# A hybrid decoder layer on one core: the order of its first column blocks, of a unit's two halves, of two norms, and the places of its tiles

## The chip, the cores and the metric

The kernel runs on one core of one Trainium2 chip. The metric is the device time of one execution in microseconds: the median of three runs before the change is 1334.2 us (1333.42 to 1334.41).

## What is computed

One layer on 256 tokens of 2048 channels, all in float32. `proj = rmsnorm(x) @ w_in` has columns for a gated-DeltaNet group (8 heads of 128: q, k, v through a causal convolution of width 4 and SiLU, a gate z, and b and a that give beta and the decay) and for a MoBA attention group (8 heads; with 256 tokens there is one block, so it is causal attention with a relative bias). The parts that the change touches:

```
q, k = l2norm(q), l2norm(k)                  # per head and token, over 128 channels
A    = tril(beta * (k k^T) * decay, -1);  T = (I + A)^-1
o_a  = rmsnorm(gated_delta_rule(q, k, v)) * silu(z);   o_b = rmsnorm(attention)
x    = x + concat(o_a, o_b) @ w_out
x    = x + cross_attention(rmsnorm(x), rmsnorm(mem))   # 4 heads, 256 memory tokens
h    = rmsnorm(x)
x    = x + (silu(dwconv3(h @ w_gate) + b) * (h @ w_up)) @ w_down      # 5632 wide
out  = rmsnorm(x)
```

## The kernel before

**Streams and units.** All weights pass one stream: a transfer on SP's queue brings a pair of units into one of three buffers `raw` (`load_pair`, line 250), and `prep` (260) splits each unit into a rounded part `hi` (ScalarE, a copy to fp32r) and a rest `lo` (VectorE, a subtraction), each in one of four tiles. `stream` (276) walks over the units, splits up to three ahead (one ahead until all of xT is there), and issues the unit's matmuls in five steps, between which `Jobs.tick` (157) may issue pieces of other work. Activations are kept channel-major as `xT`: per channel tile 256 columns of the rounded part and 256 of the rest.

A product of three terms (hi x hi, hi x rest, lo x hi) replaces each fp32 product. In a `w_unit` (296) the weights are stationary: eight matmuls of 512 columns, `hi` against both halves of an `xT` tile, then eight of 256 columns, `lo` against the rounded half. A `w_block` (325) is two such units, 16 channel tiles, and ends in an evacuation job that is added when its last `lo` matmul is issued. In an `s_block` (344) the activations are stationary and `hi` and `lo` are the moving tiles: three matmuls per channel tile and half of the tokens.

**The order of the stream** is written out from line 1144 on: the column block z0 (400 columns: b, a and three heads of z; lines 1146 and 1160), then for each head the K block and one pair of units of z1 (384 columns) or z2 (256), then Q with the MoBA values (512 columns), V with the first MoBA heads, the other MoBA heads, the keys of the memory, `w_out`, the cross-attention, the FFN in two halves of gate, up and down. The first two units of z0 hold one channel tile each, all others two.

**The jobs' order** comes from a plan: `Plan` (49) keeps a modelled time for each engine, a job is ticked when its last result is due, and evacuations wait while ScalarE or VectorE are over 3 us ahead. Tiles come from `Slots`: 14 work tiles `T`, 4 of 512 columns `T5`, 8 PSUM banks, of which side work leaves two free. On the chip each engine runs what was issued to it in that order, and semaphores make it wait.

**What the steps touch.** `start_job` (1244): splits the 16 tiles of x into `xT`, with their loads on SP's queue apart from the weight pairs (`load_x`, 1221); it loads x a second time, token-major, into `xn` (1257), squares it on ScalarE and gets the first norm r1, on which `row1` and all of the first evacuations wait. `conv_front` (555): sum of the two halves, scaling by `row1`, the convolution and SiLU, with two T tiles. `k_evac` (580): squares k on ScalarE, sums it over channels with two fp32 matmuls against `ones` (two recorded passes each) and makes the products k k^T in the same bank (597 to 601). `q_evac` (683), `v_evac` (735), `kb_evac` (829; it waits for all of U ahead of its logits), `out_norm` (711). `x_rstd` (907) sums squares over channels for the later norms. `sml` (207) holds all small parameters, those of the FFN's convolution included. When the cross-attention is over, the pool `pm` is closed and `pf` opens in its place (1325), with a filler of 96 columns ahead of `actT`.

**Where tiles lie.** The tiles of a pool lie one behind another in the order in which they are made, each rounded up to 32 bytes per partition, the pools one behind another. In the program of before, `hi0` begins at byte 45,056 of its partition, `lo0` at 61,440, `xT` at 77,824, the pool `pm` at 155,264, `oTg` at 196,224, `oTm0` at 220,800, `mT0` at 155,264 and `actT` at 155,648.

Of the kernel before, what the change touches and what calls it, by code (L numbers as in the profile page):

```python
# [16 lines left out]
P = 128  # L17
# [14 lines left out]
ZH = ((0, 3), (3, 6), (6, 8))  # L32


G_MIX, G_MEM, G_X, G_F = 0, 16, 32, 48
G_GDN, G_MOBA, C_GDN, C_FFN, B_FFN = 64, 65, 66, 66 + 96, 66 + 96 + 132
SMALL = B_FFN + FB
# [3 lines left out]
TW = 260  # L41
FILL = 96
# [136 lines left out]
class Unit:  # L179
    def __init__(self, n, ticks, after=None):  # L180
        self.n, self.ticks, self.after = n, ticks, after
# [3 lines left out]
def layer_kernel(ctx: ExitStack, tc: tile.TileContext, ins, out):  # L185
# [31 lines left out]
    stats = p0.tile([P, 640], F32, name="stats")  # L217
# [3 lines left out]
    aux = Slots(plan, [], spare=2)  # L221
# [12 lines left out]
    def stat(w, tag=None):  # L234
        _n[0] += w
        assert _n[0] <= 640
        return stats[:, _n[0] - w:_n[0]]
# [12 lines left out]
    def load_pair():  # L250
        i = state["dma"]
        if i < len(pairs):
            ap, us = pairs[i]
            n = sum(u.n for u in us)
            for a, b in ((0, us[0].n), (us[0].n, n)) if i == 0 else ((0, n),):
                sp.dma_start(raw[i % NRAW][:, a:b], ap[:, a:b])
                state[i] = state.get(i, sp.due)
            state["dma"] = i + 1

    def prep():  # L260
# [6 lines left out]
        was, plan.cur = plan.cur, Job(None, state[u.pair])  # L267
# [8 lines left out]
    def stream(upto):  # L276
        while state.setdefault("run", 0) < upto:
            i = state["run"]
            u = units[i]
            while state["prep"] <= i:  # L280
                if state[u.pair] > plan.now + AHEAD:
                    jobs.idle()
                else:
                    prep()
            plan.wait(u.due)
            for t in u.ticks:
                while (state["prep"] < min(len(units), i + 1 + (LA if (1, KT - 1) in box else 1)) and
                       state.get(units[state["prep"]].pair, 1e9) <= plan.now + AHEAD):
# [7 lines left out]
    def w_unit(src, steps):  # L296

        def high(lo_, hi_):
            def f(u):
                for j in range(lo_, hi_):  # L300
# [3 lines left out]
                    ps, w, xk = b["ps"], slice(j * P, (j + 1) * P), src(k)  # L304
                    if b["wide"]:
                        mm(ps, u.hi[:, w], xk, start=k == 0, stop=False)
                    else:
                        mm(ps[:, :256], u.hi[:, w], xk[:, :256], start=k == 0, stop=False)
                        mm(ps[:, :256], u.hi[:, w], xk[:, 256:], start=False, stop=False)
            return f  # L310

        def low(lo_, hi_):
            def f(u):
                for j in range(lo_, hi_):
                    b, k = steps[j]
                    last = k == b["k"] - 1
                    mm(b["ps"][:, :256], u.lo[:, j * P:(j + 1) * P], src(k)[:, :256], start=False, stop=last)
                    if last:
# [143 lines left out]
    def decay_job():  # L462
        ba = box["ba"].rearrange("p (b c) -> p b c", b=2)
        w = [stat(16, f"sp{i}") for i in range(6)]
# [35 lines left out]
        aux.put(ps)  # L500
        scr = dram.tile([16, P], F32, name="grow")
# [53 lines left out]
    def conv_front(ps, blk, taps, dst_fn):  # L555
# [20 lines left out]
        dst = dst_fn()  # L576
        act.activation(dst, a, AF.Silu)
        return t1, dst

    def k_evac(h):  # L580
        def f(ps):
            if "kt" not in box:
# [4 lines left out]
                box["sub"] = pm.tile([P, 2048], F32, tag="M0", name="sub")  # L587
                sp.dma_start(box["sub"][:, 1024:1536], ins["cst"][:, K_X:K_X + 512])
                box["scr"] = dram.tile([4, 2, H, 32, 32], F32, name="lscr")
                pool.memset(c[:, 2048:], 0.0)  # L590
            st = gst[h]
            t1, kT = yield from conv_front(ps, h, 4, lambda: box["kt"][:, h, :])
            act.activation(t1[:, :256], kT, AF.Square)
            yield
            while ("d", h) not in box:
                yield
            ps = yield from aux.get()
# [6 lines left out]
            vec.tensor_scalar(st[:, 0:2], ps[:, 384:386], EPS, None, op0=OP.add)  # L604
# [78 lines left out]
    def q_evac(h):  # L683
        def f(ps):
            st = gst[h]
            qT = yield from T.get()
            t1, _ = yield from conv_front(ps, 8 + h, 4, lambda: qT[:, :256])
            act.activation(t1[:, :256], qT[:, :256], AF.Square)
            yield
            while ("L", h) not in box:  # L690
                yield
            kT = box["kt"][:, h, :]
# [18 lines left out]
    def out_norm(ps, st, c_in, f_of, sink, g, z=None):  # L711

        t = yield from T.get()
# [21 lines left out]
    def v_evac(h):  # L735
        def f(ps):
            st = gst[h]
            v = yield from T.get()
            t1, _ = yield from conv_front(ps, 16 + h, 4, lambda: v[:, :256])
            T.put(t1)  # L740
# [37 lines left out]
            T.put(v)  # L778
# [23 lines left out]
            yield from out_norm(ps, st, 14, f_of, sink, gcol(G_GDN, 0), [d[:, 384:], l[:, 384:512]])  # L802
# [26 lines left out]
    def kb_evac(h):  # L829
        def f(ps):  # L830
# [3 lines left out]
            while ("qb", h) not in box or not done["bt"] or done["U"] < H:  # L834
# [25 lines left out]
            while h >= H // 2 and done["y"] < H:  # L860
                yield
            ps = yield from aux.get()
# [23 lines left out]
            yield from out_norm(ps, st, 4, f_of, sink, gcol(G_MOBA, 0))  # L886
# [19 lines left out]

    def x_rstd(ver):
# [14 lines left out]
        for tb in range(2):  # L922
            for i in range(2):
                mm(ps[:, tb:tb + 1], a[:, i * 256 + tb * P:i * 256 + (tb + 1) * P], ones[:, :1],
                   start=i == 0, stop=i == 1)
# [8 lines left out]
    def natural_ss(src, tile, ss):  # L934

        for i in range(8):
# [3 lines left out]
            plan.cur.end = sp.due  # L940
# [117 lines left out]
    def gate_evac(j):  # L1058
        def f(ps):
# [6 lines left out]
            w = sml[:, C_FFN + j * 3:C_FFN + j * 3 + 3]  # L1066
# [7 lines left out]
            act.activation(a, a, AF.Silu, bias=gcol(B_FFN, j))  # L1074
# [71 lines left out]
    def z_pairs(n):  # L1146
        us_ = s_block(xs(1), list(range(KT)), ZW[n], z_evac(n), first=0 if n else 2)
# [329 lines left out]
```

## Time and profile before

| | |
|---|---|
| runs, us | 1333.42, 1334.41, 1334.2; median 1334.2 |
| the profiled execution, us | 1333.4; its span 1331.6 |
| mean granted TensorE clock | 0.997 |
| TensorE busy, matmuls | 1316.2 us (99%) |
| VectorE, ScalarE, GpSimd busy | 938.4 (70%), 688.9 (52%), 54.7 us (4%) |
| moved by DMA | 252.53 MB, mean 190 GB/s |

Matmuls overlap in their recorded lengths: a matmul's end is modelled, and the next starts before it. What one matmul costs in a run is therefore read from start to start. All instructions bear line 96, that of a helper, so groups are told apart by their tiles: `xT,hi` is a matmul with xT moving and hi stationary. A matmul on plain fp32 tiles is recorded as two passes.

### The profile page before, as it was taken

The page shows a single profiled execution, that of the slowest core. Times are in us where ns is not written, and L with a number is a line of the kernel's source. Part 1 is how long each engine was busy: PE and PEld are TensorE (multiplying, and loading weights), DVE is VectorE, ACT ScalarE, POOL GpSimd, SP SyncE. Part 2 cuts the span into 40 slices and gives each one's busy share as a digit, 9 for nine tenths or more (in the row PEclk, how much of TensorE's full clock was granted, in tenths as well). Part 3 has the DMA queues.
Part 4 walks back from the last instruction along what each step waited for, and adds up shares of the span by engine and source line. Part 5 has one row for each costly group of instructions (what it writes and reads, how often), then busy time and mean ns, then how long its engine had stood idle before and what let it go on. Part 6 is the DMA issues. An engine that isn't in the chain of part 4 may idle for free.

```text
span 1331.6 us, 19353 instructions
## 1 busy us (share of the span) xinstructions
PE 1316.2 (99%) x7382; PEld 1147.1 (86%) x7382; DVE 938.4 (70%) x1602; ACT 688.9 (52%) x1106; POOL 54.7 (4%) x140
## 2 busy tenths in 40 slices
PE   8999999999999999999999999999999999999997
PEld 8998888888788889998888888888888888888886
DVE  5688789867686666688877777545577777775554
ACT  5776554557665454565544444443344444444443
POOL 0101000202111000000000000000000000000000
PEclk9999999999999999999999999999999999999999
DMA  9665655624355654354555666555555555555552
GB/s 332 226 226 200 226 186 190 194 80 151 123 181 191 234 193 172 145 209 167 196 192 193 200 207 205 196 197 190 189 190 190 189 190 189 190 190 190 190 190 95
DMA packets 68202, 252.53 MB, mean 190 GB/s; under 512 B 29011, under 2 KB 33292, under 8 KB 40844
## 3 DMA queue, kind: packets, MB, share of 16 engines
q1 hardware_dynamic: 66560, 247.64, 52.6%
q0 software_dynamic: 448, 2.11, 0.5%
q10 hardware_dynamic: 1100, 1.54, 0.4%
q8 instruction: 58, 0.95, 0.3%
q14 instruction: 36, 0.29, 0.1%
HBM read 246.53 MB, written 2.64 MB: 187 GB/s over the span
## 4 chain that ended last, share of the span: by engine, by line
PE 68%; issue 0%; DVE 0%; ACT 0%; POOLq 0%; POOL 0%; ACTq 0%; DVEq 0%
PE bank L96 68%; ACT xn L96 0%; DVE tt L96 0%; DVE xT L96 0%; DVE xn L96 0%; POOLq L1473 0%; POOL stats L96 0%; DVE oTx L96 0%; DVE lo L96 0%; ACT oTx L96 0%; ACTq L96 0%; DVE xres L96 0%; DVE stats L96 0%; DVEq L96 0%
## 5 line engine op out<-in xcount | busy, mean ns | idle before, releaser
L96 DVE TENSOR_TENSOR lo<-raw,hi 128x1024 fp32r<-128x1024 f32 (+4 forms) x449 | 539.9, 1204 | 315.2 <-ACT hi L96 304.9
L96 ACT ACTIVATE hi<-raw 128x1024 fp32r<-128x1024 f32 (+4 forms) x449 | 466.9, 1041 | 434.2 <-PE bank L96 329.7
L96 PE MATMUL bank<-xT,hi 128*128 128x512 f32 x2112 | 541.9, 395 | 1.4 <-DVE xT L96 1.4
L96 PEld LDWEIGHTS bank<-xT,hi 128*128 128x128 f32 x2112 | 377.8, 189 | 70.7 <-issue 2.6
L96 PEld LDWEIGHTS bank<-xT,lo 128*128 128x128 f32 x2112 | 288.0, 190 | 20.1 <-issue 0.6
L96 PE MATMUL bank<-xT,lo 128*128 128x256 f32 x2112 | 300.6, 284 | 0.0
L96 PE MATMUL bank<-hi,actT 128*128 128x512 f32 x704 | 216.9, 389 | 0.0
L96 PEld LDWEIGHTS bank<-hi,actT 128*128 128x128 f32 x704 | 132.0, 188 | 27.5
L96 PE MATMUL bank<-lo,actT 128*128 128x512 f32 x352 | 136.9, 389 | 0.0
L96 PE MATMUL bank<-hi,xT 128*128 128x512 f32 (+3 forms) x320 | 87.0, 356 | 3.5 <-ACT xT L96 2.7
L96 DVE SCALAR_TENSOR_TENSOR t<-pad,sml,t 128x256 f32<-128x256 f32 x160 | 78.2, 489 | 7.8
L96 PEld LDWEIGHTS bank<-lo,actT 128*128 128x128 f32 x352 | 66.1, 188 | 13.6
L96 ACT ACTIVATE t<-bank 128x256 f32<-128x256 f32 (+1 forms) x164 | 56.9, 350 | 26.0 <-PE bank L96 26.0
L96 PEld LDWEIGHTS bank<-hi,xT 128*128 128x128 f32 x320 | 57.7, 193 | 9.1 <-ACT xT L96 3.4
L96 DVE TENSOR_TENSOR t<-bank,t 128x256 f32<-128x256 f32 x132 | 55.0, 416 | 9.7 <-ACT t L96 9.7
L96 PE MATMUL bank<-lo,xT 128*128 128x512 f32 (+3 forms) x160 | 56.3, 352 | 0.0
L96 POOL TENSOR_TENSOR stats<-stats,pw 128x2 f32<-128x2 f32 (+1 forms) x38 | 29.0, 762 | 563.9 <-DVE stats L96 563.9
L96 ACT ACTIVATE actT<-t 128x256 fp32r<-128x256 f32 x44 | 18.2, 413 | 51.4 <-DVE t L96 51.3
L96 ACT ACTIVATE t<-t,sml 128x256 f32<-128x256 f32 x44 | 22.2, 506 | 38.9 <-DVE t L96 38.3
L96 DVE TENSOR_TENSOR t<-t,t 128x256 f32<-128x256 f32 x96 | 41.0, 427 | 1.8
L96 PEld LDWEIGHTS bank<-lo,xT 128*128 128x128 f32 x160 | 30.7, 192 | 2.6
L96 PE MATMUL bank<-oTg,hi 128*128 128x512 f32 x128 | 32.4, 395 | 0.0
(156 smaller groups left out, 984.4 us busy)
## 6 DMA issues: line engine op xcount, KB each, us to landing
raw<-wst SPq DMA_DIRECT2D x212, 1024.0 KB, 4.8
raw<-wz SPq DMA_DIRECT2D x4, 768.0 KB, 4.1
raw<-wz SPq DMA_DIRECT2D x3, 800.0 KB, 8.2
xn<-x SPq DMA_DIRECT2D x4, 512.0 KB, 10.1
raw<-wz SPq DMA_DIRECT2D x4, 512.0 KB, 4.3
tt<-mem SPq DMA_DIRECT2D x8, 256.0 KB, 5.1
tt<-memT SPq DMA_DIRECT2D x8, 256.0 KB, 5.1
xres<-xT SPq DMA_DIRECT2D x4, 512.0 KB, 5.7
```

The costliest lines, as they stand in the source:

```text
L96: r = f(o, *a, **k)
```

## The change

- **Constants and places.** The FFN's convolution weights and biases leave `sml` (338 columns become 162) for a tile `smf` of their own, loaded on GpSimd's queue when `pf` opens, ahead of `fg`. `stats` shrinks from 640 columns to 516 and is followed by a filler of 4 columns; the filler of 96 ahead of `actT` goes.
- **First columns.** z0 and z1 are interleaved unit by unit at the head of the stream, with four single-tile units each; z2's four pairs follow every second K block. Each x tile is loaded just ahead of the pair of weights that is loaded with it.
- **Turned units.** The second unit of a block runs its `lo` matmuls first; in the blocks whose halves are interleaved (memory keys, `w_out`, the first two FFN pairs) only that of every second block.
- **First norm** from squares of the channel-major x, added up and summed over channels by four one-column matmuls; the token-major load goes.
- **Norm of k** from the diagonal of k k^T: two VectorE instructions with `ident` that sum along rows, in place of the square and the two one-column matmuls.
- `conv_front` works in one T tile, jobs get their second one later; MoBA heads wait for U after their softmax and not before it; side work leaves one bank free, not two.

```diff
-SMALL = B_FFN + FB
+SMALL = C_GDN + 96
+C_FFN, B_FFN = 0, 132
+SMALL_F = B_FFN + FB
-TW = 260
-FILL = 96
+TW, STATS = 260, 516
+FILL = 4
...
-    stats = p0.tile([P, 640], F32, name="stats")
+    stats = p0.tile([P, STATS], F32, name="stats")
+    p0.tile([P, FILL], F32, name="fill")
...
-    aux = Slots(plan, [], spare=2)
+    aux = Slots(plan, [], spare=1)
...
             ap, us = pairs[i]
-            n = sum(u.n for u in us)
-            for a, b in ((0, us[0].n), (us[0].n, n)) if i == 0 else ((0, n),):
+            if i < len(x_with):
+                was, plan.cur = plan.cur, None
+                load_x(*x_with[i])
+                plan.cur = was
+            for part in [us[:1], us[1:]] if i < 2 else [us]:
+                a, b = part[0].off, part[-1].off + part[-1].n
                 sp.dma_start(raw[i % NRAW][:, a:b], ap[:, a:b])
...
         n = len(steps)
         cuts = [0, (3 * n) // 8, (6 * n) // 8, n]
-        return Unit(n * P, [high(a, b) for a, b in zip(cuts, cuts[1:])] + [low(0, n // 2), low(n // 2, n)])
-    def w_block(src, evac, wide=True):
+        hs, ls = [high(a, b) for a, b in zip(cuts, cuts[1:])], [low(0, n // 2), low(n // 2, n)]
+        return Unit(n * P, ls + hs if turn else hs + ls)
+    def w_block(src, evac, wide=True, turn=True):
         b = {"k": KT, "wide": wide, "evac": evac}
-        return [w_unit(src, [(b, k) for k in range(i, i + 8)]) for i in (0, 8)]
+        return [w_unit(src, [(b, k) for k in range(i, i + 8)], turn and i > 0) for i in (0, 8)]
...
-            t1, kT = yield from conv_front(ps, h, 4, lambda: box["kt"][:, h, :])
-            act.activation(t1[:, :256], kT, AF.Square)
+            kT = box["kt"][:, h, :]
+            t1 = yield from conv_front(ps, h, lambda: kT)
+            T.put(t1)
...
-            for tb in range(2):
-                mm(ps[:, 384 + tb:385 + tb], t1[:, tb * P:(tb + 1) * P], ones[:, :1])
             mm(ps[:, :256], kT[:, :P], kT)
             mm(ps[:, 256:384], kT[:, P:], kT[:, P:])
             yield
+            for tb in range(2):
+                stt(t1[:, tb * P:(tb + 1) * P], ps[:, tb * 256:tb * 256 + P], 1.0, ident, OP.mult, OP.mult,
+                    accum_out=st[:, tb:tb + 1])
...
-            while ("qb", h) not in box or not done["bt"] or done["U"] < H:
+            while ("qb", h) not in box or not done["bt"]:
...
-            while h >= H // 2 and done["y"] < H:
+            while done["U"] < H or (h >= H // 2 and done["y"] < H):
                 yield
...
-    for p_ in z_pairs(0):
+    for p_ in z_pairs([u for two in zip(z_units(0, Z1), z_units(1, Z1)) for u in two], 0):
         pair(*p_)
-    zp = z_pairs(1) + z_pairs(2)
+    zp = z_pairs(z_units(2, 0), KT * (ZW[0] + ZW[1]))
     for h in range(H):
         put(w_block(xs(1), k_evac(h)))
-        for p_ in zp[h:h + 1]:
+        for p_ in zp[h // 2:h // 2 + 1] if h % 2 == 0 else ():
             pair(*p_)
...
-    b = [w_block(osrc, resid_evac(n, 2, G_X, True)) for n in range(KT)]
+    b = [w_block(osrc, resid_evac(n, 2, G_X, True), turn=n % 2 > 0) for n in range(KT)]
...
+    x_with = [(0, 1), (1, 2), (2, 3), (3, 4)] + [(k, k + 2) for k in range(4, KT, 2)]
...
             if k == 11:
                 act.dma_start(sml, ins["small"])
-                xn = pm.tile([P, 2, D], F32, tag="C", name="xn")
-                for n in range(4):
-                    c = slice(n * 512, (n + 1) * 512)
-                    sp.dma_start(xn[:, :, c], ins["x"].rearrange("(b p) d -> p b d", p=P)[:, :, c])
+            if k % 2:
+                t = yield from T5.get()
...
+                    act.activation(t, xraw[:, k - 1:k + 1, :].rearrange("p b c -> p (b c)"), AF.Square)
+                    yield
+                    vec.tensor_tensor(sq, sq, t, op=OP.add)
+                    T5.put(t)
...
+        ps = yield from acc.get()
+        token_sums(ps, sq)
...
     pf = ctx.enter_context(tc.tile_pool(name="pf", bufs=1))
-    pf.tile([P, FILL], F32, name="fill")
     box["actT"] = pf.tile([P, HB, 512], F32R, name="actT")
     fg = pf.tile([P, D], F32, name="fg")
+    box["smf"] = pf.tile([P, SMALL_F], F32, name="smf")
+    pool.dma_start(box["smf"], ins["smallf"])
```

## Rows read from the trace of the kernel before

**Rows 1.** The page's first part: busy time of each engine, its share of the span, and its number of instructions.

```profile
PE 1316.2 (99%) x7382; PEld 1147.1 (86%) x7382; DVE 938.4 (70%) x1602; ACT 688.9 (52%) x1106; POOL 54.7 (4%) x140
```

**Rows 2.** Busy time by stage, in four stretches: from the first column block to its end, the K stage, the stage of Q and of the MoBA values, and the stage of V with the attention heads. Columns: stretch (us), its length, then busy us and number of instructions of TensorE's matmuls, of its weight loads, of VectorE, ScalarE and GpSimd, the granted TensorE clock (1.00 is 2.4 GHz), the mean busy share of the DMA engines, and GB/s.

```profile
5.50:29.08 23.58, 20.19 (x96) 19.23 (x97) 15.77 (x27) 14.92 (x25) 0.00 (x0) 0.93 0.98 355
29.08:106.16 77.08, 77.08 (x473) 70.34 (x473) 57.41 (x134) 50.82 (x89) 6.43 (x15) 1.00 0.67 240
106.16:207.76 101.60, 101.60 (x547) 87.95 (x545) 86.13 (x161) 58.14 (x101) 9.32 (x21) 1.00 0.56 195
207.76:393.50 185.74, 185.74 (x1136) 158.69 (x1135) 144.20 (x332) 114.46 (x263) 25.74 (x44) 1.00 0.44 153
```

**Rows 3.** The timeline of TensorE's matmuls over the first 30 us. Columns: start (us), length with the modelled end (us), engine, helper line, operation, output and operands (moving first, then stationary), array size, columns, number of matmuls merged, and in brackets the idle time before them with what ended it.

```profile
5.50 1.23 PE L96 MATMUL bank<-hi,xT 128*128 128x400 f32 x2
...
6.75 0.52 PE L96 MATMUL bank<-hi,xT 128*128 128x400 f32 x2
...
7.29 0.52 PE L96 MATMUL bank<-hi,xT 128*128 128x400 f32 x2
...
11.21 0.45 PE L96 MATMUL bank<-hi,xT 128*128 128x400 f32 x1 [2.67 <-ACT xT L96]
...
12.37 0.45 PE L96 MATMUL bank<-hi,xT 128*128 128x400 f32 x1 [0.71 <-DVE xT L96]
...
29.08 2.02 PE L96 MATMUL bank<-xT,hi 128*128 128x512 f32 x8
```

**Rows 4.** The timeline of TensorE's matmuls (columns as before): first the first and the last start of a run of 24 matmuls of 256 columns in the third column block, then the first and the last start of a run of 18 matmuls of 512 columns in the down projection.

```profile
75.06 0.40 PE L96 MATMUL bank<-hi,xT 128*128 128x256 f32 x2
...
77.94 0.63 PE L96 MATMUL bank<-xT,hi 128*128 128x512 f32 x2
...
909.82 0.39 PE L96 MATMUL bank<-lo,actT 128*128 128x512 f32 x1
...
913.90 0.39 PE L96 MATMUL bank<-lo,actT 128*128 128x512 f32 x1
```

**Rows 5.** The timeline of TensorE's matmuls in the FFN's gate and up blocks: the start of one unit, of its second half, and of the unit three further on.

```profile
821.17 2.00 PE L96 MATMUL bank<-xT,hi 128*128 128x512 f32 x8
823.02 1.11 PE L96 MATMUL bank<-xT,lo 128*128 128x256 f32 x8
...
829.55 2.00 PE L96 MATMUL bank<-xT,hi 128*128 128x512 f32 x8
```

**Rows 6.** The timeline of TensorE's matmuls in the output projection: a unit on oTm, the start of the next unit and of its second half, and the unit four after the first.

```profile
431.76 2.02 PE L96 MATMUL bank<-oTm,hi 128*128 128x512 f32 x8
...
434.56 2.03 PE L96 MATMUL bank<-oTm,hi 128*128 128x512 f32 x8
436.42 1.12 PE L96 MATMUL bank<-oTm,lo 128*128 128x256 f32 x8
...
443.00 1.31 PE L96 MATMUL bank<-oTg,hi 128*128 128x512 f32 x5
```

**Rows 7.** The timeline of ScalarE around 9 us, and then busy time, clock and DMA of three short stretches (columns as in the rows by stage).

```profile
9.13 0.87 ACT L96 ACTIVATE hi<-raw 128x800 fp32r<-128x800 f32 x1 [2.88 <-DMA raw<-wz]
...
0.00:12.00 12.00, 7.70 (x31) 6.48 (x31) 4.25 (x11) 5.80 (x10) 0.20 (x4) 1.00 0.81 262
...
8.35:11.21 2.86, 0.19 (x3) 0.00 (x1) 1.18 (x2) 2.08 (x4) 0.00 (x0) 1.00 1.01 392
...
14.00:16.00 2.00, 2.00 (x7) 1.98 (x7) 2.00 (x5) 1.57 (x3) 0.00 (x0) 0.50 1.04 396
```

**Rows 8.** Groups of instructions on VectorE and ScalarE, shapes kept apart. Columns: line, engine, operation, output and operands, shapes, count, busy us, mean ns of one, and idle time before them with what ended it.

```profile
L96 DVE TENSOR_TENSOR lo<-raw,hi 128x800 fp32r<-128x800 f32 x7 | 6.8, 990 | 4.4 <-ACT hi L96 4.3
L96 DVE TENSOR_TENSOR tt<-tt,tt 128x512 f32<-128x512 f32 x14 | 9.5, 681 | 0.0
L96 DVE SCALAR_TENSOR_TENSOR AB<-bank,stats,AB 128x128 f32<-128x128 f32 x16 | 5.5, 341 | 0.0
L96 ACT ACTIVATE hi<-raw 128x800 fp32r<-128x800 f32 x7 | 6.0, 867 | 4.7 <-DMA raw<-wz 3.6 <-PE bank L96 0.9
```

**Rows 9.** DMA issues of the page: output and source, queue, count, KB of each, and median us from issue to landing.

```profile
xn<-x SPq DMA_DIRECT2D x4, 512.0 KB, 10.1
```

**Rows 10.** The timeline of TensorE's matmuls: first a head's k work inside a K block, then the sums over channels ahead of the FFN.

```profile
96.88 0.50 PE L96 MATMUL bank<-ones,t 128*128 128x1 f32 x4
97.24 0.90 PE L96 MATMUL bank<-kt 128*128 128x256 f32 x4
97.89 0.71 PE L96 MATMUL bank<-xT,hi 128*128 128x512 f32 x2
...
609.40 0.94 PE L96 MATMUL bank<-ones,tt 128*128 128x1 f32 x8
610.21 0.96 PE L96 MATMUL bank<-xT,lo 128*128 128x256 f32 x6
```

**Rows 11.** The timeline of TensorE's matmuls in the first column block: two starts that lie 24 matmuls apart.

```profile
20.39 0.53 PE L96 MATMUL bank<-hi,xT 128*128 128x400 f32 x2
...
24.74 0.53 PE L96 MATMUL bank<-hi,xT 128*128 128x400 f32 x2
```

**Rows 12.** The timeline of GpSimd, and then of VectorE, around the start of the FFN.

```profile
589.29 0.63 POOL L96 DMA_DIRECT2D fg<-fg  x1 [69.11 <-DVE xres L96]
...
617.38 0.34 DVE L96 TENSOR_SCALAR t<-pad,sml 128x256 f32<-128x256 f32 x1
```

More of the change, by code (lines that the diff above doesn't have):

```diff
@@ L266, in prep @@
         h, l = hi[i % NRING][:, :u.n], lo[i % NRING][:, :u.n]
-        was, plan.cur = plan.cur, Job(None, state[u.pair])
+        was, plan.cur = plan.cur, Job(None, u.at)
         act.activation(h, src, AF.Copy)
@@ L280, in stream @@
             while state["prep"] <= i:
-                if state[u.pair] > plan.now + AHEAD:
+                if units[state["prep"]].at > plan.now + AHEAD:
                     jobs.idle()
@@ L287, in stream @@
                 while (state["prep"] < min(len(units), i + 1 + (LA if (1, KT - 1) in box else 1)) and
-                       state.get(units[state["prep"]].pair, 1e9) <= plan.now + AHEAD):
+                       units[state["prep"]].at <= plan.now + AHEAD):
                     prep()
@@ L316, in f @@
                     last = k == b["k"] - 1
-                    mm(b["ps"][:, :256], u.lo[:, j * P:(j + 1) * P], src(k)[:, :256], start=False, stop=last)
-                    if last:
+                    mm(b["ps"][:, :256], u.lo[:, j * P:(j + 1) * P], src(k)[:, :256], start=False,
+                       stop=last and not turn)
+                    if last and not turn:
                         jobs.add(b["evac"](b["ps"]))
@@ L463, in decay_job @@
         ba = box["ba"].rearrange("p (b c) -> p b c", b=2)
-        w = [stat(16, f"sp{i}") for i in range(6)]
+        sp_t = yield from T.get()
+        w = [sp_t[:, i * 16:(i + 1) * 16] for i in range(6)]
         v = [t.rearrange("p (b c) -> p b c", b=2) for t in w]
@@ L500, in decay_job @@
         aux.put(ps)
+        T.put(sp_t)
         scr = dram.tile([16, P], F32, name="grow")
@@ L737, in f @@
             st = gst[h]
-            v = yield from T.get()
-            t1, _ = yield from conv_front(ps, 16 + h, 4, lambda: v[:, :256])
-            T.put(t1)
+            v = yield from conv_front(ps, 16 + h)
             yield
@@ L905, in resid_evac, with token_sums @@
         return f
+    def token_sums(ps, a):
+        for tb in range(2):
+            for i in range(2):
+                mm(ps[:, tb:tb + 1], a[:, i * 256 + tb * P:i * 256 + (tb + 1) * P], ones[:, :1],
+                   start=i == 0, stop=i == 1)
     def x_rstd(ver):
@@ L921, in x_rstd @@
         ps = yield from aux.get()
[L922 to L925, printed above, removed]
+        token_sums(ps, a)
         T5.put(a)
@@ L939, in natural_ss @@
             sp.dma_start(t, src[tb * P:(tb + 1) * P, n * 512:(n + 1) * 512])
-            plan.cur.end = sp.due
+            plan.cur.end = sp.due + 5.0
             yield
@@ L1144, in layer_kernel, with z_pairs @@
     wz, wst = ins["wz"], ins["wst"]
[L1146 to L1148 removed]
+    def z_pairs(us_, o):
+        ps = []
         for i in range(0, len(us_), 2):
@@ L1153, in z_pairs, with z_units @@
         return ps
+    def z_units(n, first):
+        return s_block(xs(1), list(range(KT)), ZW[n], z_evac(n), first=first)
     def put(us):
@@ L1181, in msrc @@
         return when(("m", k), lambda: box["m", k])
-    b = [w_block(msrc, mk_evac(h)) for h in range(XH)]
+    b = [w_block(msrc, mk_evac(h), turn=h % 2 > 0) for h in range(XH)]
     us += [u[0] for u in b] + [u[1] for u in b]
@@ L1245, in start_job @@
         for k in range(KT):
-            plan.cur.end = xdue[k]
+            while len(xdue) <= k:
+                yield
+            plan.cur.end = xdue[k] - (MARGIN if k == 0 else 0.0)
             yield
```

99 lines of the change are left out of this document (52 added, 47 removed).

## The prediction

> **What bounds the kernel now.** I read the busy shares first. TensorE is busy for 1316.2 of 1331.6 us [rows 1]; a share says nothing yet about pace, so next come the stages, where TensorE is busy throughout from 29 to 393 us while VectorE is below 85% [rows 2]. In that whole stretch a step hidden on VectorE, ScalarE or a queue is worth nothing. Two kinds of time are left. One is idle time: it lies in the first 20 us [rows 3]. The other is the spacing of matmuls, read from start to start in the timeline of TensorE, since their modelled ends overlap. In long runs of one width the spacing is constant: 24 matmuls of 256 columns in 2.88 us, 120.0 ns each, and 18 of 512 columns in 4.08 us, 226.7 ns each [rows 4]. A unit of eight 512s and eight 256s would take 2.774 us at these; in the FFN it takes (829.55-821.17)/3 = 2.793 us [rows 5]. The eight 512s that follow 256s take 1.85 us there against 1.81: a change of width costs 0.02 us a unit. Where the moving tile is oTg or oTm, four units take 443.00-431.76 us, 2.810 each, and eight 512s take 1.86 us, 232.5 ns each [rows 6]: same shapes, other tiles, another pace.
>
> **Part 1, interleaved first columns.** The first 96 matmuls (400 columns) run from 5.50 to 29.08 us. At the pace of 6.75 to 7.29, 180 ns, they need 17.3 us, so 6.3 are lost. The first three, waiting for the first token tile, lose 0.7 (1.25 us against 0.54); that stays. Then TensorE stands still for 2.67 us up to 11.21, and for 0.71 up to 12.37 [rows 3], because ScalarE waited 2.88 us for a weight transfer that began to be used at 9.13 [rows 7]; the DMA engines are at 1.01 busy and 392 GB/s. After that pause the granted clock is 0.50 (1.2 GHz) around 14 to 16 us. So 5.6 us are open. The change gives every token tile two column blocks to work on: 6x(180+173) ns = 2.1 us of TensorE per tile (the second block, 384 columns, by 384/400) in place of 1.08, for 128+392 KB of DMA in place of 128+200. That is 250 GB/s against 310; the first 12 us moved 262 GB/s on average, 3.1 MB [rows 7]. What must be there before the fifth pair of units is, with that pair, 3.2 MB, at about 12.2 us and a little more for the constants; then come 0.87 and 0.99 us of splitting [rows 8], and TensorE wants it at 6.2+4x2.1 = 14.7. It is tight, and the ring of three buffers holds the fifth pair's issue back until the second is split: I allow 1 us of stall. Term: -4.6 (ends -2.5 and -5.6). Every x tile now passes the SP queue just ahead of its pair; the queue waits there for VectorE as it does now. The moved block leaves the K stage, which only moves work TensorE does anyway.
>
> **Part 2, first norm.** The four 512 KB transfers of natural x go [rows 9], which nothing on TensorE waits for after 20 us: nothing gained there, but less DMA. Eight ScalarE squares of 512 columns stay squares (now of xT), seven VectorE adds of 681 ns are new [rows 8], in a stage where VectorE is 67% busy (15.77 of 23.58 us, [rows 2]): hidden; without that cover 4.8 us. Four one-column fp32 matmuls are new: the same four in the FFN take 610.21-609.40 = 0.81 us [rows 10]. Term +0.8 on TensorE.
>
> **Part 3, norm of k from its Gram matrix.** Per head four recorded passes of one column go: 97.24-96.88 = 0.36 us [rows 10], eight heads, -2.9. The kt matmuls behind them take 97.89-97.24 = 0.65 us, the first of them perhaps longer for following a one-column pass; I allow as much as one more such pass, 0.09 us a head, for that (ends -2.9 and -3.6). VectorE gets 16 instructions of 128x128 at 341 ns, 5.5 us [rows 8], and ScalarE loses eight squares. VectorE has 57 of 77 us in use there [rows 2]; hidden as long as the splits ahead of TensorE keep their lead of three units.
>
> **Part 4, turned units.** The second unit of a block runs its 256s first, so two 256 runs and two 512 runs meet. Of 152 blocks, 128 stand alone and each saves one pair of width changes; mk, w_out and the first two FFN pairs, where only odd blocks turn, add 12, of which 10 work on oTg, oTm or mT, which don't show the steady pace: I count 130. One pair costs 2.793-2.774 = 0.0195 us [rows 4, 5]. Term -2.5 (ends 0 and -2.7). The wait this moves: a turned unit needs its lo tile 1.85 us sooner. VectorE's splits run up to three units ahead, so I put it at nothing; if it were late, all matmuls behind it would wait.
>
> **Part 5, the tiles' places.** Tiles lie one behind another, each rounded up to 32 bytes. Now hi0, lo0, xT and actT start at 45,056, 61,440, 77,824 and 155,648, all multiples of 4,096; oTg, oTm and mT lie 128 past a multiple of 256. The change takes 704 bytes out of sml, so raw, hi, lo and xT all start 704 lower: hi0 at 44,352, 64 past a multiple of 128. FILL and STATS put the tiles of the second pool, then actT, at 154,112, a multiple of 512. So xT keeps its place against hi and lo, and actT loses its place. No row shows both operands 64 off. With one off by 128 (oTg) the 512s take 232.5 instead of 226.7: +5.8 ns on 1056 matmuls of the down projection would be +6.1. With the moving one 64 past a multiple of 128 in every second unit (second token tile of a 400-column unit, 1,600 bytes in), 24 matmuls take 24.74-20.39 = 4.35 us, 181.3 ns against 180 [rows 3, 11]: +1.3 ns, or 1.7 at 512 columns. The offset is this one's, so I take it: +1.7 on actT (ends 0 and +6.1; a gain has no row), nothing on xT, nothing for oTg, which stays off against hi.
>
> **Part 6, the rest.** One T tile less per head, the later wait for U in the MoBA heads, the split of sml and the spare bank move work on VectorE and ScalarE, with TensorE at 100% above it [rows 2]: nothing; if the plan got worse there, TensorE would show gaps. The new POOL transfer of the FFN constants goes ahead of fg, which was issued at 589.29; the first use of those constants is at 617.38 [rows 12]: 28 us of cover. Behind a late one stand VectorE and the splits.
>
> **Sum.** The profiled execution took 1333.4 us (span 1331.6 and 1.8 around it). 1333.4-4.6+0.8-2.9-2.5+1.7 = 1325.9. The median of the runs shown is 0.8 higher, so **1326.7 us**.
>
> **Rivals.**
> (a) Places cost nothing at all: 1333.4-4.6+0.8-2.9-2.5 = 1324.2, 1325.0 as a median. Against it: the oTg rows beside the FFN rows. Chance 0.17. The Trainium skill, TensorE: Matmul & The Clock Gate, in What happens when you issue a matmul, gives TensorE two independent read ports, so that loading the next weights takes nothing from the running matmul; by that rule this rival holds. The trace does not agree with it fully: 226.7 and 232.5 ns stand for one shape.
> (b) Slower: **what counts is each operand's own multiple**, and all of hi, lo, xT fall off it. Every xT unit then takes the oTg unit's 2.810 us instead of 2.793: 264 units, +4.5, and turning gains nothing; the down projection +6.1, the 192 MoBA value matmuls of 512 columns +1.1. 1333.4-4.6+0.8-2.9+4.5+6.1+1.1 = 1338.4, 1339.2 as a median. For it: hi, lo and xT do move off 4,096; against it: moving and stationary move together. It decides from about 3 ns on the 3,360 matmuls of 512 columns. Chance 0.16.
> (c) Only actT pays the full 5.8 ns: 1333.4-4.6+0.8-2.9-2.5+6.1 = 1330.3, 1331.1 as a median. Chance 0.13.
> (d) The start stays bound by transfers, since the three buffers hold less per load (392 KB a pair), and gives 1 us: 1329.5, 1330.3 as a median. For it: DMA at 1.01 busy [rows 7]. Against: fewer bytes per TensorE time, 250 GB/s for 310. Chance 0.09.
> The forecast keeps 0.45.
>
> **Numbers.** About 0.2%, 2.7 us, can be told from no change: below 1331.5 is faster, above 1336.9 slower. Faster: forecast, (a), (d) and about half of (c), less some for a plan that came out worse, 0.72. Slower: (b), 0.16. Same: 0.12. The range is 1321.5 to 1334: below, (a) with the start at -5.6 and k at -3.6 (1322.4, 1323.2 as a median) and a little more; above, (c) with a weak start; (b) is left out.
>
> **What would show it.** Right: no TensorE pause between 8 and 12 us, the clock at 1.00 from there on, the first two column blocks done by about 41 us; blocks in the FFN of 5.57 us instead of 5.59; no one-column matmuls between k's; down-projection matmuls at 227 to 229 ns. Wrong: 512-column spacing of 230 ns or more on xT, pauses of TensorE that end with VectorE's lo between 40 and 110 us, or a pause at the fifth pair.

## The result, and the profile after

The changed kernel takes 1323.96 us (median of four runs, 1322.6 to 1326.43), the kernel before 1333.81 in the same comparison: a ratio of 0.9933, 95% interval 0.992 to 0.9945, so 9.9 us less. The profiled execution took 1323.5 us, its span 1321.7.

The page's first part, which answers to [rows 1]:

```profile
PE 1308.6 (99%) x7358; PEld 1140.1 (86%) x7358; DVE 941.4 (71%) x1643; ACT 685.2 (52%) x1092; POOL 51.5 (4%) x141
```

**The start.** Busy time by stretch, columns as in [rows 2]: the first two column blocks, and two of the stretches of [rows 7]; then the timeline of TensorE as in [rows 3].

```profile
4.63:40.99 36.36, 35.76 (x195) 33.65 (x194) 28.61 (x45) 25.88 (x46) 0.00 (x0) 1.00 0.85 304
0.00:12.00 12.00, 10.64 (x51) 8.97 (x52) 5.45 (x15) 7.98 (x17) 0.20 (x4) 1.00 0.79 261
...
14.00:16.00 2.00, 1.60 (x9) 1.16 (x8) 1.30 (x2) 2.00 (x4) 0.00 (x0) 1.00 0.90 343
```

```profile
4.63 0.61 PE L100 MATMUL bank<-hi,xT 128*128 128x400 f32 x2
...
5.40 0.52 PE L100 MATMUL bank<-hi,xT 128*128 128x400 f32 x2
...
14.76 0.58 PE L100 MATMUL bank<-hi,xT 128*128 128x400 f32 x2
15.74 0.45 PE L100 MATMUL bank<-lo,xT 128*128 128x400 f32 x1 [0.40 <-DVE lo L100]
```

No pause between 8 and 12 us; a short one at the fifth pair (0.98 us from 14.76 to 15.74 where 0.36 is the pace); the clock stays at 1.00 between 14 and 16 us, where it was 0.50. The transfers move 261 GB/s in the first 12 us, as before: TensorE does 10.64 us of work with them instead of 7.70. The first matmul starts at 4.63 us, 0.87 earlier than before, and the first three take 0.77 us instead of 1.25.

**The norms.** The timeline of TensorE: the sums over tokens of the first norm, and two heads' Gram matrices in one burst ([rows 10]).

```profile
44.28 0.94 PE L100 MATMUL bank<-ones,tt 128*128 128x1 f32 x8
45.09 0.72 PE L100 MATMUL bank<-xT,lo 128*128 128x256 f32 x4
...
95.82 1.47 PE L100 MATMUL bank<-kt 128*128 128x256 f32 x8
97.04 1.17 PE L100 MATMUL bank<-xT,hi 128*128 128x512 f32 x4
```

The sums take 45.09-44.28 = 0.81 us. A head's k work takes (97.04-95.82)/2 = 0.61 us instead of 1.01.

**The long runs.** "512s" and "256s" are matmuls of 512 and of 256 columns. Timeline of TensorE: one block of the FFN from run of 256s to run of 256s ([rows 5]); seven steps of three matmuls of the down projection ([rows 4]); the output projection ([rows 6]).

```profile
800.61 2.08 PE L100 MATMUL bank<-xT,lo 128*128 128x256 f32 x16
...
806.17 2.08 PE L100 MATMUL bank<-xT,lo 128*128 128x256 f32 x16
```

```profile
903.53 0.62 PE L100 MATMUL bank<-hi,actT 128*128 128x512 f32 x2
...
908.34 0.62 PE L100 MATMUL bank<-hi,actT 128*128 128x512 f32 x2
```

```profile
410.84 2.03 PE L100 MATMUL bank<-oTg,hi 128*128 128x512 f32 x8
412.71 1.07 PE L100 MATMUL bank<-oTg,lo 128*128 128x256 f32 x8
413.62 2.02 PE L100 MATMUL bank<-oTg,hi 128*128 128x512 f32 x8
```

A block on xT takes 5.56 us (two units of 2.793 before). A step of the down projection takes (908.34-903.53)/7 = 687 ns instead of 680: the two matmuls that move hi take 230.5, the one that moves lo 226. On oTg the 512s still take (412.71-410.84)/8 = 234 ns, but the 256s (413.62-412.71)/8 = 114 instead of 119.

Summed from start to start over whole classes, after less before: the first two column blocks and the earlier first matmul -4.7 us, k's one-column passes -2.7 and its kt matmuls -0.6, the token sums +0.8, 512s on xT -2.6 and 256s +0.4, down projection +2.3, 256s on oTg and oTm -1.2. That is -8.3 of -9.9. The other 1.6 are spread over smaller classes: the block on mem is 1.2 us shorter (a wait of 0.96 us in it became one of 0.40), and the small fp32 matmuls of the attention heads lie in another order. No run isolates these 1.6.

### The profile page after: what moved, and what is told of

It is laid out like the page before. It is cut to its first block, busy times and chain, and to the rows that moved or that the text cites. A ratio compares the mean times of both kernels' runs of the same rounds, so it can differ in the third digit from the quotient of the medians.

```text
span 1321.7 us, 19344 instructions
## 1 busy us (share of the span) xinstructions
PE 1308.6 (99%) x7358; PEld 1140.1 (86%) x7358; DVE 941.4 (71%) x1643; ACT 685.2 (52%) x1092; POOL 51.5 (4%) x141
## 4 chain that ended last, share of the span: by engine, by line
PE 95%; DMA 1%; DVE 1%; issue 1%; ACT 1%; SPq 0%; ACTq 0%; POOLq 0%; POOL 0%; DVEq 0%
PE bank L100 95%; ACT hi L100 1%; DMA sub<-lscr 1%; DVE lo L100 1%; DMA raw<-wz 0%; SPq L100 0%; DMA lscr<-AB 0%; DVE t L100 0%; DVE tt L100 0%; ACT xn L100 0%; DVE xT L100 0%; ACT t L100 0%; DVE xn L100 0%; ACTq L100 0%; DVE sub L100 0%
## 5 line engine op out<-in xcount | busy, mean ns | idle before, releaser
L100 DVE TENSOR_TENSOR lo<-raw,hi 128x1024 fp32r<-128x1024 f32 (+3 forms) x452 | 539.3, 1196 | 309.3 <-ACT hi L100 307.3
L100 ACT ACTIVATE hi<-raw 128x1024 fp32r<-128x1024 f32 (+3 forms) x452 | 468.4, 1038 | 423.9 <-PE bank L100 372.3
L100 PE MATMUL bank<-xT,hi 128*128 128x512 f32 x2112 | 521.8, 394 | 1.4 <-DVE xT L100 1.4
L100 PEld LDWEIGHTS bank<-xT,hi 128*128 128x128 f32 x2112 | 385.0, 188 | 75.4 <-DVE xT L100 2.2
L100 PEld LDWEIGHTS bank<-xT,lo 128*128 128x128 f32 x2112 | 271.5, 191 | 11.8 <-issue 1.2
L100 PE MATMUL bank<-xT,lo 128*128 128x256 f32 x2112 | 279.9, 284 | 0.0
L100 DVE SCALAR_TENSOR_TENSOR t<-pad,smf,t 128x256 f32<-128x256 f32 x88 | 42.7, 485 | 6.4 <-DVE t L100 0.5
L100 ACT ACTIVATE t<-t,smf 128x256 f32<-128x256 f32 x44 | 22.2, 504 | 45.4 <-DVE t L100 45.4
L100 DVE SCALAR_TENSOR_TENSOR t<-pad,sml,t 128x256 f32<-128x256 f32 x72 | 35.1, 489 | 2.1 <-ACT t L100 0.3
```

The source lines that it names most:

```text
L100: r = f(o, *a, **k)
```

## The experiments

All but before_xT_64 are edits of the changed kernel and are compared with its 1323.96 us. The runs of one kernel spread by up to 3.8 us, and one cause showed itself: the start, the same program in all of these kernels but old_start and before_xT_64, had its first two column blocks done at anything from 40.6 us (pm_64) to 44.8 us (spare_wait). So beside each total I read the spacing of the stage in question, which repeats to 0.1%.

**no_turn.**

```
-        return [w_unit(src, [(b, k) for k in range(i, i + 8)], turn and i > 0) for i in (0, 8)]
+        return [w_unit(src, [(b, k) for k in range(i, i + 8)]) for i in (0, 8)]
```

Expected: 

> The changed kernel with every second unit run as in the kernel before (512s first, then 256s); all else as changed. Theory (turning saves two changes of width per block): units on xT go back to 2.793 us, blocks in the FFN from 5.57 to 5.59 us, about 2.2 us more in all: 1326.2 us. Rival (the gain on xT came from the tiles' places): nothing changes, 1324.0 us. Second question: the 256s on oTg and oTm, 113 ns in the changed kernel against 119 before: if that came with the places, they stay at 113; if with the turned units, they go back to 119 and the time is 1.2 us longer still, 1327.4 us.

Measured: 1322.54 us (1322.35 to 1324.62), 1.4 less; the ranges of the two kernels overlap. Timeline of the FFN, two units apart:

```profile
802.22 2.00 PE L100 MATMUL bank<-xT,hi 128*128 128x512 f32 x8
...
807.81 2.00 PE L100 MATMUL bank<-xT,hi 128*128 128x512 f32 x8
```

The units on xT did go back to 2.793 us, and the 256s on oTg stayed at 113. So the spacing term is real and the places, not the turning, gave oTg its 113. But the kernel did not become slower. Timeline of TensorE at the end of the cross attention, where oTx moves against its output weights (w_xo), first of the changed kernel, then of no_turn:

```profile
555.83 1.99 PE L100 MATMUL bank<-tt,kv 128*128 128x256 f32 x8 [0.30 <-ACT kv L100]
...
558.36 2.19 PE L100 MATMUL bank<-oTx,hi 128*128 128x256 f32 x15 [0.43 <-DVE oTx L100]
...
561.33 2.05 PE L100 MATMUL bank<-oTx,hi 128*128 128x256 f32 x16
...
564.16 2.05 PE L100 MATMUL bank<-oTx,hi 128*128 128x256 f32 x16
```

```profile
561.85 1.98 PE L100 MATMUL bank<-oTx,hi 128*128 128x256 f32 x16
...
564.57 1.98 PE L100 MATMUL bank<-oTx,hi 128*128 128x256 f32 x16
```

The waits that end with kv and oTx, and two more of 0.29 and 0.40 us just before 162 and 404 us, are in the changed kernel and not in no_turn: 1.4 us. The runs of 256s behind them go at 2.83/24 = 118 ns instead of 2.72/24 = 113, one program text and the same places in both kernels. So turning wins 2.2 us on xT, and behind the first two column blocks no_turn's profiled execution is still 1.8 us shorter. Not all of that is turning's doing: of the waits only the 0.43 us that ends with oTx stands in every kernel with turned units (and in none without), and w_xo goes at 113 ns in five other kernels with turned units (xT_128, xT_64, k_ones, old_start, spare_wait).

**pm_at_hi.** `FILL = 4` becomes `FILL = 212`.

Expected: 

> The changed kernel with the second pool (mT, oTg, oTm, actT) moved up by 832 bytes, so that actT and oTg start at the same place modulo 4,096 as hi, lo and xT; nothing else. Theory R (what counts is the place of the moving tile against the stationary one): the down projection's matmuls that move hi go from 230.5 back to 226.7 ns, 704 of them: -2.5 us; in the output projection 512s go from 233 to 227 and 256s from 113 to 120, which cancel: 1321.7 us. Theory M, of the prediction (the moving tile's own place, 64 past a multiple of 128, costs): hi has not moved, they stay at 230.5, 1324.0 us.

Measured: 1323.43 us (1322.23 to 1325.49). Timeline of the down projection, six steps, then of the start:

```profile
900.03 0.62 PE L100 MATMUL bank<-hi,actT 128*128 128x512 f32 x2
...
904.11 0.61 PE L100 MATMUL bank<-hi,actT 128*128 128x512 f32 x2
```

```profile
14.16 0.34 PE L100 MATMUL bank<-lo,xT 128*128 128x384 f32 x1
16.29 0.94 PE L100 MATMUL bank<-hi,xT 128*128 128x400 f32 x2 [1.79 <-ACT hi L100]
```

```profile
16.00:18.00 2.00, 1.62 (x4) 1.08 (x5) 1.46 (x3) 1.89 (x4) 0.00 (x0) 0.61 1.02 411
18.00:20.00 2.00, 2.00 (x8) 1.98 (x7) 2.00 (x3) 1.54 (x3) 0.00 (x0) 0.54 1.12 396
```

A step is back at (904.11-900.03)/6 = 680 ns, and the down projection 2.4 us shorter: theory R. Theory M is refuted, hi having kept its own place. The total doesn't show it, because in this execution the pause at the fifth pair lasted 1.79 us and the clock (stretch rows above) was near half speed for the next 4 us: the first two blocks were done at 43.7 us instead of 41.0. The output projection's 512s went to 227 and its 256s to 120, 0.5 us more.

**xT_128** and **xT_64.** An empty tile between lo and xT, of 32 columns for xT_128 and of 16 for xT_64; FILL is 104 and 120, so that the pools behind keep their place modulo 512 against hi.

```
+    p0.tile([P, 32], F32, name="gap")
     xT = p0.tile([P, KT, 512], F32R, name="xT")
```

Expected, xT_128: 

> The changed kernel with 128 empty bytes between lo and xT, and the pools behind moved 512 in all, so that only the place of xT against hi and lo changes. Theory R: units on xT take the pace of oTg before the change (512s 232.5, 256s 119 ns, 2.810 us a unit) and turning gains nothing: 264 units by 0.017 and the 2.2 us of turning, and 192 matmuls that move 512 columns of hi by 5.8 ns: 1331 to 1333 us. Theory M, or places that don't matter: 1324.0 us.

Expected, xT_64: 

> The same with 64 empty bytes (the pools behind again 512 further). Theory R, any difference of place counts: 512s at 230 to 233 ns; 256s at 113 (as on oTg in the changed kernel, where the difference is 192) give 2.77 us a unit and 1324 to 1326 us, 256s at 119 give 1331 to 1333 us. If only multiples of 128 or more count, 226.7 and 120 ns stay, 1324.0 us.

Measured: xT_128 1331.44 us (1329.6 to 1333.19), xT_64 1319.47 us (1318.13 to 1320.44). Timeline of the FFN, one block of xT_128, then two blocks of xT_64:

```profile
801.72 2.06 PE L100 MATMUL bank<-xT,lo 128*128 128x256 f32 x16
...
807.34 2.06 PE L100 MATMUL bank<-xT,lo 128*128 128x256 f32 x16
```

```profile
799.82 3.84 PE L100 MATMUL bank<-xT,hi 128*128 128x512 f32 x16
...
810.86 1.32 PE L100 MATMUL bank<-xT,hi 128*128 128x512 f32 x5
```

A unit takes 2.81 us at a distance of 128 and 11.04/4 = 2.76 at 64, against 2.783. Both are theory R. For 64 the better of its two branches comes nearest, but the time lies 4.5 us below that branch's range: the 256s went from 120 to 113 in some runs and 118 in the others, the 512s only from 227 to 230.

The MoBA values use the same two tiles the other way round: there hi moves and xT stands. Timeline of xT_64, four steps of three matmuls:

```profile
111.60 0.63 PE L100 MATMUL bank<-hi,xT 128*128 128x512 f32 x2
...
114.40 0.63 PE L100 MATMUL bank<-hi,xT 128*128 128x512 f32 x2
```

These 512s take (114.40-111.60)/12 = 233 ns, so it matters which of the two tiles moves.

**k_ones.**

```
             t1 = yield from conv_front(ps, h, lambda: kT)
-            T.put(t1)
+            act.activation(t1[:, :256], kT, AF.Square)
...
+            for tb in range(2):
+                mm(ps[:, 384 + tb:385 + tb], t1[:, tb * P:(tb + 1) * P], ones[:, :1])
             mm(ps[:, :256], kT[:, :P], kT)
...
-                stt(t1[:, tb * P:(tb + 1) * P], ps[:, tb * 256:tb * 256 + P], 1.0, ident, OP.mult, OP.mult,
-                    accum_out=st[:, tb:tb + 1])
```

Expected: 

> The changed kernel with the norm of k computed as before (ScalarE squares k, eight times two one-column fp32 matmuls with ones); all else as changed. Theory (those passes lie on TensorE's path): 32 recorded passes come back at 84 ns, 2.7 us, and the kt matmul behind them takes about 0.07 us longer in each of eight heads: 3.3 us, 1327.3 us. Rival (the two reads of the Gram matrix that VectorE no longer does, and the shorter wait of the bank, are worth as much): 1324.0 us.

Measured: 1329.69 us (1328.66 to 1332.1), 5.7 more. The passes themselves came back at 2.7 us and the kt matmuls at 0.6, as expected. 3.2 us more stand in a stage that has none of them, that of V and the attention heads. Rows of that stage, the changed kernel's first, then k_ones's:

```profile
201.19:385.05 183.86, 183.77 (x1140) 159.06 (x1139) 149.10 (x354) 114.58 (x272) 26.29 (x48) 1.00 0.44 157
```

```profile
204.78:391.87 187.09, 186.64 (x1147) 159.58 (x1145) 151.67 (x353) 116.68 (x276) 27.58 (x48) 1.00 0.44 156
```

Six of its 377 small matmuls have come from the block on mem (0.6 us shorter); all 377 take 115 ns on average, the changed kernel's 371 took 111, in another order among the weights' units; the weights' own matmuls take 1.0 us more. Why that order is slower I did not isolate.

**old_start.** The old order of blocks, x transfers and wz:

```
-    for p_ in z_pairs([u for two in zip(z_units(0, Z1), z_units(1, Z1)) for u in two], 0):
+    for p_ in z_pairs(z_units(0, 2), 0):
         pair(*p_)
-    zp = z_pairs(z_units(2, 0), KT * (ZW[0] + ZW[1]))
+    zp = z_pairs(z_units(1, 0), KT * ZW[0]) + z_pairs(z_units(2, 0), KT * (ZW[0] + ZW[1]))
...
+        load_x(n)
+    load_x(NRAW)
```

Expected: 

> The changed kernel with the first column blocks as before: the 400 columns alone first, then 384 columns between the blocks of k, the old order of the x transfers and of wz; the first norm stays that of the channel-major tokens. Theory (the first twelve us are bound by transfers): a pause of TensorE of 2 to 3.5 us near 11 us, the granted clock at 0.50 after it, and 4.7 us more: 1328.7 us. Rival (the start waits for the same bytes anyway, as its fifth pair does now for up to 2 us): 1 to 2 us more, 1325.5 us.

Measured: 1327.7 us (1327.17 to 1328.4), 3.7 more. Timeline of TensorE and two stretches:

```profile
10.95 0.45 PE L100 MATMUL bank<-hi,xT 128*128 128x400 f32 x1 [2.46 <-ACT xT L100]
12.12 0.55 PE L100 MATMUL bank<-hi,xT 128*128 128x400 f32 x1 [0.71 <-DVE xT L100]
```

```profile
12.00:14.00 2.00, 1.89 (x6) 1.86 (x7) 1.77 (x4) 2.00 (x5) 0.00 (x0) 0.58 1.06 429
14.00:16.00 2.00, 2.00 (x8) 1.98 (x8) 2.00 (x5) 2.00 (x4) 0.00 (x0) 0.57 1.02 399
```

The pause and the half clock are back. Up to the end of the K stage it is 4.7 us longer; the stage of V is 1.7 us shorter than in the changed kernel, again the same work in another order.

**places** (both moves, FILL 200) and **places_no_turn** (and no turned units).

Expected, places: 

> Both moves of places at once: xT 64 bytes behind hi's place, and the second pool at hi's place modulo 4,096. If the spacing follows from the difference of place of the two operands of each matmul: the 1319.5 us of xT_64 less the 2.4 us that the down projection gave in pm_at_hi: 1317.1 us, with the output projection 0.5 us longer in it. Rival (what the spacing does depends on what ran before): the two don't add up, 1319.5 us.

Expected, places_no_turn: 

> The same without turned units. If a change of width costs at this place too: FFN blocks take 0.02 us more, 2.1 us in all, and the waits of 1.4 us that only kernels with turned units show (before 162, 404, 556 and 558 us) go: 1317.8 us. If a change of width costs nothing where the operands differ in place, only the waits go: 1315.7 us.

Measured: places 1319.13 us (1317.91 to 1319.69), places_no_turn 1315.96 us (1315.59 to 1316.87), a ratio to before of 0.9871, 0.9858 to 0.9885. In places each stage does what it did in the kernel with one move (gate and up as in xT_64, down at 680 ns a step), yet the total gained only 0.3: the output projection, the cross attention and w_xo, whose 256s went from 113 to 120, took 2.0 us more, against 2.3 less in the down projection. Timeline of the FFN in places_no_turn, two units apart:

```profile
801.34 2.00 PE L100 MATMUL bank<-xT,hi 128*128 128x512 f32 x8
...
806.86 2.00 PE L100 MATMUL bank<-xT,hi 128*128 128x512 f32 x8
```

2.76 us a unit without turning, as with it: at this place a change of width costs nothing, the waits (0.8 us in places) are gone, and this is the fastest version I ran, 8.0 us below the changed kernel. Of the 3.2 us between it and places the waits and a start done 0.8 us sooner make up half; the rest is spread over the stages with small jobs, so that 1315.7 was met in part by luck.

**before_xT_64.** The kernel before with the same 64 empty bytes and nothing else (its fill 80 instead of 96).

Expected: 

> The kernel before with one edit: 64 empty bytes between lo and xT (its fill ahead of actT 64 less, so that actT stays at hi's place; oTg, oTm, mT come to 192 past it). No turned units, old start, old norms. If the place of xT against hi and lo sets the spacing by itself: gate and up 6.1 us shorter (as places_no_turn against before), the other 88 units on xT 3.0 us, the 256s on oTg and oTm 1.2 us, the values' 512s 1.1 us longer: 9.2 us less than before, 1324.4 us. Rival (the gain needs something else of the change): 1333.6 us.

Measured: 1324.55 us (1324.02 to 1325.32), ratio 0.9936 (0.9923 to 0.9948). Timeline of the FFN, two units apart, 2.76 us each:

```profile
799.89 2.00 PE L96 MATMUL bank<-xT,hi 128*128 128x512 f32 x8
...
805.41 2.00 PE L96 MATMUL bank<-xT,hi 128*128 128x512 f32 x8
```

Gate and up were 3.1 us shorter in each half, the output projection 1.2, w_xo 1.0; the first column block took 1.5 longer in the profiled execution. By itself the place does what was expected of it, and 64 empty bytes are worth as much as the whole change, whose ratio is 0.9933.

**spare_wait.**

```
-    aux = Slots(plan, [], spare=1)
+    aux = Slots(plan, [], spare=2)
...
-            while ("qb", h) not in box or not done["bt"]:
+            while ("qb", h) not in box or not done["bt"] or done["U"] < H:
...
-            while done["U"] < H or (h >= H // 2 and done["y"] < H):
+            while h >= H // 2 and done["y"] < H:
```

Expected: 

> The changed kernel with two spare banks kept back for the small jobs' start instead of one, and the MoBA heads waiting for U at their old, earlier place. By the prediction's part 6 these are worth nothing: 1324.0 us. Rival (the 1.9 us that the stage of V and the attention heads lost, and part of the 1.2 us of the block on mem, came with them): 1325.5 to 1327 us, that stage back at 185.7 us.

Measured: 1338.97 us (1338.22 to 1341.24), 15.0 more: both expectations missed. The block on mem, and three of the waits in it (timeline of TensorE):

```profile
388.44:429.03 40.59, 31.97 (x159) 26.54 (x158) 25.79 (x60) 18.43 (x42) 3.91 (x7) 0.83 0.39 139
```

```profile
392.63 0.50 PE L100 MATMUL bank<-mT,hi 128*128 128x512 f32 x1 [1.51 <-DVE mT L100]
...
395.21 0.79 PE L100 MATMUL bank<-mT,hi 128*128 128x512 f32 x1 [1.86 <-DVE mT L100]
...
417.77 1.22 PE L100 MATMUL bank<-mT,hi 128*128 128x512 f32 x2 [2.43 <-DVE mT L100]
```

The block takes 40.6 us instead of 25.8; TensorE waits for mT, and the granted clock is 0.83 over it. So the heads' later wait and the smaller spare are not free of effect in the changed kernel. They are not slow by themselves: the kernel before has both old settings, and its block on mem takes 27.0 us; they cost that much only together with something else of the change. Which of the two does it, and with what, was not separated, and the stage of V didn't lengthen to 185.7 (184.5).

**pm_256** and **pm_64**, one run each: FILL = 20 and 104.

Expected, pm_256: 

> The changed kernel with the second pool 64 bytes up, so that actT, oTg and oTm lie 256 past hi's place modulo 512 (192 before). If multiples of 256 count as the same place: the down projection's three matmuls a step at 226.7 each, 680 ns in all, the output projection's 256s at 120. If only multiples of 512: 687 ns and 113 or 119 as now.

Expected, pm_64: 

> The changed kernel with the second pool 384 bytes up, so that actT, oTg and oTm lie 64 past hi's place modulo 512. If what xT_64 showed goes by the difference of place and not by the tile: the output projection's units (eight 512s and eight 256s) at 2.76 us instead of 2.774, the four groups 22.07 us each instead of 22.19; down projection 687 ns a step or less. If it goes by the tile: 22.19 us, no change.

Measured: 1322.23 and 1326.77 us. Timeline of the output projection, two units apart, pm_256 and pm_64, then nine steps of the down projection in pm_64:

```profile
413.36 2.00 PE L100 MATMUL bank<-oTg,hi 128*128 128x512 f32 x8
...
418.94 2.00 PE L100 MATMUL bank<-oTg,hi 128*128 128x512 f32 x8
```

```profile
412.60 2.00 PE L100 MATMUL bank<-oTg,hi 128*128 128x512 f32 x8
...
418.12 1.99 PE L100 MATMUL bank<-oTg,hi 128*128 128x512 f32 x8
```

```profile
825.85 0.63 PE L100 MATMUL bank<-hi,actT 128*128 128x512 f32 x2
...
832.15 0.63 PE L100 MATMUL bank<-hi,actT 128*128 128x512 f32 x2
```

At 256 the pace is that of no distance: 2.79 us a unit, 120 ns for 256s, 680 ns a step of the down projection. At 64 the output projection takes 2.76 a unit, as xT did at 64. But the down projection, all 512s, went to 233 ns a matmul, 700 a step: there I expected 687 or less and was wrong. The direction of the distance accounts for it. In the output projection oTg moves and hi stands, in the down projection hi moves and actT stands. Counted from the start of the stationary tile to that of the moving one, modulo 256, a pool that lies 64 past hi is at 64 for oTg but at 192 for actT, and in the changed kernel, whose pool lies 192 past hi, it is the other way round. Read so, 64 gave 229 to 230 ns (xT in xT_64, oTg in pm_64, and actT in the changed kernel with 687/3 = 229), and 192 gave 233 (oTg in the changed kernel, actT in pm_64, the MoBA values in xT_64).

## Why the prediction came out as it did

The forecast of 1326.7 lay 2.7 us above the 1323.96 measured, inside the range, and faster was likeliest. Point by point:

**Start** (-4.6): right as to the mechanism, [rows 3, 7] answered by a timeline without a pause of over 0.2 us up to 15 us. The size, -4.7 in this execution, is in part luck: 1.3 of it come from the earlier first matmul and from the first three matmuls, which the sum held fixed. Rival (d) did not hold here, but it names what spoils it elsewhere: in three of the experiments with this same start (pm_at_hi, xT_128, spare_wait) the pause at the fifth pair took 1.8 us or more and the two blocks ended 2.7 to 3.7 us later. I allowed one such microsecond as fixed; it is a spread.

**Token sums** (+0.8): 0.81.

**Norm of k** (-2.9, ends to -3.6): -3.3 on the matmuls themselves. The kt matmuls behind did give their share, 0.6, which I had left in the bound. Undoing it alone cost 5.7: 3.2 us more stand in a stage without k's passes, where the order of the small jobs had changed; no term had that.

**Turned units** (-2.5): the size of the spacing was right, -2.2. Yet no_turn is no slower. The wait that I put at nothing, for the lo tile, is indeed not there: behind 20 us no pause of the changed kernel ends with lo. What was missing is a term for the small jobs, which fall elsewhere when units are turned and wait there. And 0.0195 us for a change of width holds only where the operands lie at one place.

**Places** (+1.7 on actT): +2.3, near, but for a wrong reason. I took the moving tile's own offset of 64 as the cause; pm_at_hi left that offset and the cost was gone. What counts is the distance between the two operands of a matmul. The row that gave me the price [rows 11] has that distance too, hi's second token tile moving 64 past xT, which may be why the size came near. With xT moved by 64 it turns round: in the last four units of 400 columns the first token tile's matmuls take 180.0 ns and the second's 181.2 in the changed kernel, 182.6 and 180.3 in places_no_turn. "Nothing for oTg" failed for the same reason: it went from a distance of 128 to 192, the 256s sped up by 5 ns, -1.2. Rival (b) failed because hi, lo and xT moved together: a unit of 2.81 us, its price, did appear as soon as xT moved alone by 128. Rival (c)'s 5.8 ns on every actT matmul was reached, and passed with 6.7, only where the pool lies 64 past hi (pm_64).

Rival (a), that places cost nothing, failed too: moving xT by 64 or 128 bytes changed the time by -4.5 or +7.5 us. The Trainium skill, TensorE: Matmul & The Clock Gate, in What happens when you issue a matmul, gives TensorE two independent read ports, so that loading the next weights takes nothing from the running matmul; that the two tiles' places are then indifferent does not agree with these runs.

**The rest** (0): the step with the least working and the largest miss. I costed Part 6 at nothing because TensorE was at 100% above it, but TensorE at 100% is not TensorE doing it in a fixed time: the stage of V and the attention heads took from 182.1 us (old_start, with 358 small matmuls in it) to 187.1 us (k_ones, with 377), with the same 768 weights' matmuls, and spare_wait showed 15 us behind two of its edits. The 1.6 us that my terms don't explain are left for this part by elimination; no run shows where they come from.

Where the missing 2.7 us are: 1.2 on oTg and oTm, 1.6 in the rest, 0.4 on k and 0.1 at the start, against 0.6 more on actT and 0.3 less from turning; that is 2.4, and the remaining 0.3 is how the two profiled executions stand to their medians.

## What to carry to other kernels

Read the matmul's spacing from start to start for each pair of tiles, and look up where the two tiles lie against each other before planning anything finer: in this kernel an empty tile of 64 bytes did as much as all parts of the change together. An engine at 100% does not make the work scheduled beside it free; where a hand-made planner orders it, every edit also reshuffles, and single edits undone do not add up to the change. Where a start runs against its transfers, quote its gain as a spread and judge other edits by their own stage.

## What the hardware showed that I had not expected

In these runs the spacing of fp32r matmuls goes by the distance from the start of the stationary tile to that of the moving one, modulo 256 bytes; distances of 0, 64, 128, 192 and 256 were run. Nanoseconds for 512 and for 256 columns, and a unit of eight of each without turning or, where marked, with it:

| distance | 512 columns | 256 columns | unit, us | seen in |
|---|---|---|---|---|
| 0 (and 256) | 226.7 | 120.0 | 2.793, turned 2.783 | xT before and after, pm_256 |
| 64 | 229 to 230 | 113 or 118 | 2.757, turned 2.759 | xT_64, places_no_turn |
| 128 | 232 | 119 | 2.810, turned 2.811 | oTg before, xT_128 |
| 192 | 233 | 113 or 118 | 2.773, turned the same | oTg in no_turn and after (its 256s at 113) |

Only 512s lose by a distance and 256s gain by one, so work that is all 512s wants none: 680 ns a step of the down projection at 0, 687 at 64, 700 at 192. At 64 and at 192 runs of 256s go at 113 or at 118 with the same tiles (w_xo, at 192, in no_turn and in the changed kernel), and what picks one of the two is open. So is why the place matters at all: the runs show the paces and no mechanism.
